# A two-layer hybrid decoder trunk on one core: four edits to its seams — low parts first in the opening, memory rows by halves of the contraction, the last output columns in two banks, queries scaled on ScalarE

## The chip, the core and the metric

One NeuronCore of a Trainium2 chip runs the whole program. The metric is the device time of one execution in microseconds (us), lower is better. Engines are named as in the profile: PE (TensorE, matrix products), ACT (ScalarE), DVE (VectorE), POOL (GpSimd) and SP (SyncE, which issues nearly all DMAs).

## The reference, cut to what matters

A sequence of 256 tokens of width 1024 goes through two layers, all in float32:

```python
for layer in range(2):
    x = x + 0.5 * swiglu(rms_norm(x), w_gate, w_up, w_down)      # 1024 -> 2816 -> 1024
    h, mem_n = rms_norm(x), rms_norm(mem)                        # mem: 256 rows of 1024
    mix = mlstm_mixer(h, mem_n, ...) if layer == 0 else dilated_mixer(h, mem_n, k_sh, v_sh, ...)
    x = x + mix                                                  # both hold a memory cross-attention
    x = x + 0.5 * swiglu(rms_norm(x), w_gate, w_up, w_down)
    if layer == 0: k_sh, v_sh = normed keys, values of rms_norm(x) @ w_kv
```

The memory cross-attention normalises queries and keys per head (4 heads of 64), takes a softmax over the 256 memory rows, and multiplies by the memory's values. Keys and values are `mem_n @ w_mem_kv`, 512 columns. The mLSTM mixer has 4 heads, the dilated mixer 12 heads in 3 groups.

## The kernel before, in words

**Exact products from split operands.** Each float32 weight and each activation is split into a high part (rounded to the fast float32 form that TensorE takes) and a low part, the remainder. ACT writes the high part (`hi`, a cast), DVE the low part (`lo`, a subtraction). A product of a 128x128 block with up to 512 columns is three matmuls into one PSUM bank: high with low, high with high, low with high (`mm3`, lines 561 to 566). In the trace the first name behind the arrow is the weight (`hi` or `lo`), the second the activation (`xh`, `xl`).

**Weight units.** `_stream` (line 54) lists all weights in the order of use, as units of at most 128 x 1024. SP loads a unit into one of 6 `raw` buffers, ACT and DVE split it into one of 8 ring slots (`RING`), and PE uses it twice, once for each half `t` of the 256 tokens. `release` (line 547) counts the uses and frees slots in the order of the stream only: a unit that is held keeps the slots of all units behind it.

**The planner.** No hardware scheduler orders the program. While it is recorded, a small model of the engines (`_Model`, line 167) keeps a clock for each engine, and side jobs (`spawn`: activations, norms, softmax, transposes) are recorded into the engines' queues when that clock says they are due. Each engine then runs its queue in order and waits on semaphores. `PAUSE` (line 38) is a number of microseconds that the planner adds between the scaling of a softmax row on DVE and its transposes on PE; it is not a wait on the chip.

**Opening.** The first product (`opening`, line 741) has nothing to hide behind: for each of 8 blocks `k` of the contraction it casts x's two halves (`xh`), casts the weights (`hi`), then records on DVE the weights' low part and x's two low parts (`xl`), and six matmuls. Unit 0 comes in two loads of half the width (`parts`, line 490), the others in one.

**Memory.** `memory` (line 71) puts six units in the stream behind the fifth feed-forward block: two of the transposed memory (`memT`, one for each half of the memory's rows, all 8 contraction blocks in each; POOL multiplies a gain into them) and four of weights (`mkv`, two contraction blocks each). `memory_kv` (line 910) goes over the four weight units, and in each over both halves of rows `m`, with one PSUM bank for each half. The bank is taken over from the feed-forward block before (`bank_of`). `keys` then norms the keys (ACT squares, DVE sums, POOL takes the power -1/2, DVE scales), and PE transposes them (`tpk`).

**Queries.** `query_rms` (line 686) serves both mixers: ACT squares the projected queries out of PSUM, DVE scales them into SBUF (`qn`), PE transposes them (`tpq`). Two PSUM banks (`tp`) serve all transposes, four (`acc`) the accumulators and scores, two (`mm`) the projections.

**End.** Every feed-forward ends in `dn` (line 867): eleven blocks accumulate into two banks of 512 columns for each half of tokens; after the last block DVE adds half of the bank to x, and SP stores 128 x 512 of the output. For the second half of tokens the last two products are those of columns 512 to 1023.

Of the kernel before, what the change touches and what calls it, by code (L numbers as in the profile page):

```python
# [17 lines left out]
P = 128  # L18
D = 1024
# [18 lines left out]
PAUSE = 1.0  # L38
# [13 lines left out]
def _stream():  # L52
# [285 lines left out]
class _Kernel:  # L338
# [151 lines left out]
    def parts(self, i):  # L490

        n = self.units[i][2]
        return [slice(0, n // 2), slice(n // 2, n)] if i == 0 else [slice(0, n)]

    def emit_unit(self):
# [6 lines left out]
        def steps(raw):  # L502
            if key[0] == "memT":
                raw3 = raw.rearrange("p (k t) -> p k t", k=NK)
                self.nc.gpsimd.tensor_tensor(
                    raw3, raw3, self.gains[7 + key[1]].unsqueeze(2).to_broadcast([P, NK, P]), ALU.mult)
                yield
# [178 lines left out]
    def query_rms(self, src, n, q, out, rstd):  # L686
# [5 lines left out]
        nc.vector.tensor_scalar(q, src, rstd, None, ALU.mult)  # L692
# [49 lines left out]
    def opening(self, ps, key):  # L742
# [4 lines left out]
        for k in range(NK):  # L747
# [14 lines left out]
            nc.vector.tensor_tensor(wl, raw[:, s], wh.bitcast(F32), ALU.subtract)  # L762
            for t, (hi, lo) in enumerate(parts):
                nc.vector.scalar_tensor_tensor(lo, x[:, t * P:(t + 1) * P], g, hi.bitcast(F32),
                                               ALU.mult, ALU.subtract)
            for t, (hi, lo) in enumerate(parts):
                self.matmul(ps[t], hi, wh, k == 0, False)
            for t, (hi, lo) in enumerate(parts):
                self.matmul(ps[t], hi, wl, False, False)
            for t, (hi, lo) in enumerate(parts):  # L770
                self.matmul(ps[t], lo, wh, False, k == NK - 1)
# [25 lines left out]
    def ffn_in(self, layer, which, after, memory, fp):  # L797
# [68 lines left out]

        def dn(b, t):
            if len(acc) == t:
# [6 lines left out]
            pairs = [(c, h) for h in range(2) for c in range(2)] if last else \  # L875
                    [(c, h) for c in range(2) for h in range(2)]
            for n, (c, h) in enumerate(pairs):
                wh, wl = self.get("dn", layer, which, b, c)
                self.until(max(self.model.ready(a) for a in (wl, parts[c][1])))
                f = slice(h * 512, (h + 1) * 512)  # L880
                self.mm3(acc[t][h], parts[c], (wh[:, f], wl[:, f]),
                         b == 0 and c == 0, last and c == 1)
                if last and n % 2:
                    nc.vector.scalar_tensor_tensor(self.x[t][:, f], acc[t][h], 0.5, self.x[t][:, f],
                                                   ALU.mult, ALU.add)
                    after(t, h)
                if h == 1:
# [33 lines left out]
    def memory_kv(self, layer, pool):  # L921
# [22 lines left out]
        ps, xT = [], []  # L944
        for k in range(0, NK, 2):
            for m in range(2):
                if k == 0:
                    ps.append(self.bank_of(m))
                    xT.append([a.rearrange("p (k t) -> p k t", k=NK)
                               for a in self.get("memT", layer, m)])  # L950
                hi, lo = xT[m]
                wh, wl = self.get("mkv", layer, k)
                self.until(self.model.ready(wl))
                for j in range(2):
                    s = slice(j * 512, (j + 1) * 512)
                    self.mm3(ps[m], (hi[:, k + j, :], lo[:, k + j, :]), (wh[:, s], wl[:, s]),
                             k + j == 0, k + j == NK - 1)
                self.release("mkv", layer, k)
                if k + 2 == NK:
                    self.release("memT", layer, m)  # L960
                    self.holder[m] = self.spawn(keys(m)(ps[m]))
                    chains.append(self.holder[m])
                self.tick()
# [534 lines left out]
    def run(self, stop=None):  # L1498
# [41 lines left out]
        def store(t, h):  # L1540
            f = slice(h * 512, (h + 1) * 512)
# [35 lines left out]
def _arrays(inputs):  # L1577
# [16 lines left out]
    w["memT"] = np.ascontiguousarray(w["mem"][0].reshape(2, P, NK, P).transpose(0, 3, 2, 1)).reshape(2 * P, D)  # L1594
# [23 lines left out]
```

## Time and profile before

| | |
|---|---|
| time, median of 3 runs | 1000.31 us (1000.02 to 1000.97) |
| the profiled execution: time / span of its instructions | 1000.46 us / 998.7 us |
| PE busy | 984.3 us, 99% of the span, clock 1.0 throughout |
| DVE / ACT / POOL busy | 628.3 / 550.3 / 65.0 us |
| DMA | 205 MB, mean 205 GB/s |

The span runs from the first instruction to the last; the profiled execution's time has 1.8 us more around it. A row of the timeline has a start, a duration, the engine, the line and the tiles; a bracket at its end tells how long the engine had been idle before it, and who ended that. Matmuls overlap: a row of 128x512 lasts 0.39 us, but the next one starts 0.23 us after it, and "idle" counts only from the modelled end.

### The profile page before, as it was taken

What the parts mean: (1) busy time and instruction counts of PE and PEld (TensorE: products, weight loads), DVE (VectorE), ACT (ScalarE), POOL (GpSimd) and SP (SyncE); (2) the same over time, 40 slices, a digit from 0 to 9 for tenths busy, and PEclk for the clock granted to TensorE, in tenths of its full rate; (3) what the DMA queues carried; (4) which work ended last, traced back from release to release, by engine and by line L of the source; (5) the groups of instructions that cost most, each with busy time, mean ns of one, the idle gap of its engine ahead of it and who ended that gap; (6) DMA issues with size and microseconds to landing.
All of it is one profiled execution on the core that took longest, in us unless ns stands there. A gap on an engine that the chain in (4) does not pass through costs nothing.

```text
span 998.7 us, 12959 instructions
## 1 busy us (share of the span) xinstructions
PE 984.3 (99%) x4673; PEld 814.2 (82%) x4673; DVE 628.3 (63%) x922; ACT 550.3 (55%) x853; POOL 65.0 (7%) x82
## 2 busy tenths in 40 slices
PE   9999999999999999999999999999999899999998
PEld 6887888898998888888877888788887688888886
DVE  5855656567967755556568563765567875665652
ACT  7655545478785644535377554554556585453541
POOL 0002000010010000000023010200012000000000
PEclk9999999999999999999999999999999999999999
DMA  9966867355446667676538675867551346767651
GB/s 361 306 207 219 292 225 216 118 158 196 153 149 210 199 224 259 207 246 206 199 109 305 232 237 174 290 206 253 175 192 64 106 161 219 263 208 242 211 172 42
DMA packets 80008, 205.05 MB, mean 205 GB/s; under 512 B 7564, under 2 KB 28744, under 8 KB 79944
## 3 DMA queue, kind: packets, MB, share of 16 engines
q1 hardware_dynamic: 79800, 204.20, 61.0%
q8 instruction: 36, 0.59, 0.2%
q14 instruction: 28, 0.23, 0.1%
q10 hardware_dynamic: 144, 0.04, 0.0%
HBM read 193.17 MB, written 11.03 MB: 204 GB/s over the span
## 4 chain that ended last, share of the span: by engine, by line
PE 82%; DVE 3%; POOL 2%; ACT 2%; issue 1%; DMA 1%; DVEq 0%; ACTq 0%
PE gups L567 42%; PE acc L567 22%; PE aps L567 7%; PE oacc L567 3%; PE kvps L567 2%; PE bqps L567 2%; DVE lo L277 1%; PE tps L574 1%; POOL rp_r L277 1%; DVE s L277 1%; PE sc L567 1%; PE po L567 1%; DMA hd<-hb 1%; POOL rp_e L277 1%; PE tpp L574 0%
## 5 line engine op out<-in xcount | busy, mean ns | idle before, releaser
L277 DVE TENSOR_TENSOR lo<-raw,hi 128x1024 fp32r<-128x1024 f32 (+3 forms) x351 | 407.1, 1181 | 125.9 <-ACT hi L277 119.3
L277 ACT CAST hi<-raw 128x1024 fp32r<-128x1024 f32 (+3 forms) x351 | 350.6, 1019 | 143.7 <-PE acc L567 84.4
L567 PE MATMUL gups<-lo,xh 128*128 128x512 f32 x704 | 273.8, 391 | 0.9 <-DVE lo L277 0.9
L567 PE MATMUL gups<-hi,xh 128*128 128x512 f32 x704 | 272.9, 389 | 1.0 <-ACT hi L277 1.0
L567 PE MATMUL gups<-hi,xl 128*128 128x512 f32 x704 | 272.7, 389 | 0.0
L567 PEld LDWEIGHTS gups<-lo,xh 128*128 128x128 f32 x704 | 132.0, 188 | 29.5 <-DVE lo L277 1.6
L567 PEld LDWEIGHTS gups<-hi,xh 128*128 128x128 f32 x704 | 132.0, 188 | 29.1 <-ACT hi L277 2.2
L567 PEld LDWEIGHTS gups<-hi,xl 128*128 128x128 f32 x704 | 132.2, 188 | 27.7
L277 ACT ACTIVATE sil<-gups,rstd 128x256 f32<-128x256 f32 x88 | 41.6, 474 | 163.9 <-PE gups L567 159.3
L277 DVE SCALAR_TENSOR_TENSOR h<-gups,rstd,sil 128x256 f32<-128x256 f32 x88 | 42.2, 481 | 123.6 <-ACT sil L277 123.5
L567 PE MATMUL acc<-lo,hhb 128*128 128x512 f32 x304 | 119.6, 393 | 0.0
L567 PE MATMUL acc<-hi,hlb 128*128 128x512 f32 x304 | 118.5, 390 | 0.0
L567 PE MATMUL acc<-hi,hhb 128*128 128x512 f32 x304 | 118.3, 389 | 0.0
L567 PEld LDWEIGHTS acc<-hi,hlb 128*128 128x128 f32 x304 | 57.1, 188 | 12.0
L567 PEld LDWEIGHTS acc<-hi,hhb 128*128 128x128 f32 x304 | 57.1, 188 | 11.4
L567 PEld LDWEIGHTS acc<-lo,hhb 128*128 128x128 f32 x304 | 57.1, 188 | 11.3
L567 PE MATMUL aps<-lo,xh 128*128 128x384 f32 (+1 forms) x144 | 49.5, 344 | 0.0
L567 PE MATMUL aps<-hi,xh 128*128 128x384 f32 (+1 forms) x144 | 47.5, 330 | 0.0
L567 PE MATMUL aps<-hi,xl 128*128 128x384 f32 (+1 forms) x144 | 47.5, 330 | 0.0
L277 DVE STREAM_TRANSPOSE hb<-h 128x256 f32<-128x256 f32 x76 | 33.6, 442 | 15.5 <-DMA hd<-hb 14.5
L277 POOL TENSOR_SCALAR rstd<-ss 128x1 f32<-128x1 f32 x12 | 3.6, 303 | 500.1 <-ACT junk L277 500.1
L277 ACT CAST hhb<-ht 128x512 fp32r<-128x512 f32 x38 | 23.6, 621 | 20.2 <-DMA ht<-hd 19.5
(189 smaller groups left out, 1012.9 us busy)
## 6 DMA issues: line engine op xcount, KB each, us to landing
raw<-in_wts SPq DMA_DIRECT2D x311, 512.0 KB, 4.7
raw<-in_wts SPq DMA_DIRECT2D x32, 384.0 KB, 3.8
hd<-hb SPq DMA_DIRECT2D x38, 256.0 KB, 5.3
ht<-hd SPq DMA_DIRECT2D x38, 256.0 KB, 4.6
bias<-diag SPq DMA_DIRECT2D x1, 1536.0 KB, 7.2
xraw<-in_xT SPq DMA_DIRECT2D x4, 256.0 KB, 6.2
x<-in_x SPq DMA_DIRECT2D x2, 512.0 KB, 8.5
mt<-in_mem SPq DMA_DIRECT2D x2, 512.0 KB, 6.9
```

The source lines that it names most:

```text
L277: call(out, *args, **kw)
L567: self.pe.matmul(out, lhsT=lhsT, rhs=rhs, start=start, stop=stop)
L574: self.pe.transpose(out, in_, ident)
```

## The change

Four edits and a number.

1. `opening`: DVE does x's low parts ahead of the weights' low part, and PE takes the products in the order that fits; unit 1 is loaded in two halves too.
2. `memory` and `memory_kv`: a `memT` unit now holds four contraction blocks of all 256 rows, and is followed in the stream by the two weight units that it meets. Each half of the contraction is finished for both halves of rows before the next.
3. `dn`: in the last feed-forward, for the second half of tokens, columns 512 to 1023 close their bank one block earlier and are added to x; the last block's product goes to two new banks of 256 columns, each with its own addition and store.
4. `query_rms`: queries are scaled on ACT instead of DVE.
5. `PAUSE` is 1.5 instead of 1.0.

```diff
-PAUSE = 1.0
+PAUSE = 1.5
     def memory(layer):
-        for m in range(2):
-            units.append((("memT", layer, m), ("memT", None, None, m, 1), D))
-        single(("mkv", layer), "w_mem_kv", layer, 0, 512, 2)
+        for q in range(2):
+            units.append((("memT", layer, q), ("memT", None, None, q, 1), D))
+            for k in range(4 * q, 4 * q + 4, 2):
+                units.append((("mkv", layer, k), (None, layer, (("w_mem_kv", 0, 512),), k, 2), 1024))
...
-        return [slice(0, n // 2), slice(n // 2, n)] if i == 0 else [slice(0, n)]
+        return [slice(0, n // 2), slice(n // 2, n)] if i < 2 else [slice(0, n)]
...
-        nc.vector.tensor_scalar(q, src, rstd, None, ALU.mult)
+        nc.scalar.activation(q, src, AF.Copy, scale=rstd)
...
             nc.scalar.copy(wh, raw[:, s])
-            nc.vector.tensor_tensor(wl, raw[:, s], wh.bitcast(F32), ALU.subtract)
             for t, (hi, lo) in enumerate(parts):
                 nc.vector.scalar_tensor_tensor(lo, x[:, t * P:(t + 1) * P], g, hi.bitcast(F32),
                                                ALU.mult, ALU.subtract)
+            nc.vector.tensor_tensor(wl, raw[:, s], wh.bitcast(F32), ALU.subtract)
...
+            groups = [(slice(h * 512, (h + 1) * 512), acc[t][h], b == 0, last) for h in range(2)]
+            if (layer, which, t) == (1, 2, 1) and b >= NB - 2:
+
+                f, a, begins, _ = groups.pop()
+                if last:
+                    self.freed_bank(*self.holder)
+                    add(t, f, a)
+                    for lo in (512, 768):
+                        bank = self.mm.tile([P, 512], F32, tag="mm", name="end")
+                        groups.append((slice(lo, lo + 256), bank[:, :256], True, True))
+                else:
+                    groups.append((f, a, begins, True))
...
+        for q in range(2):
+            hi, lo = (a.rearrange("p (k t) -> p k t", k=4) for a in self.get("memT", layer, q))
             for m in range(2):
...
+                for k in range(4 * q, 4 * q + 4, 2):
+                    wh, wl = self.get("mkv", layer, k)
...
+                    self.release("mkv", layer, k)
...
+            self.release("memT", layer, q)
```

The planner turns these edits into other orders. Three places, in the order in which each engine's queue holds its instructions:

The first instructions of DVE in the opening, before and then now; `lo` is the weights' low part, `xl` x's low part for one half of the tokens.

```order
L277 TENSOR_TENSOR lo_150<-raw_113,hi_149 128x512
L277 SCALAR_TENSOR_TENSOR xl_146<-xraw,gains,xh_145 128x128
L277 SCALAR_TENSOR_TENSOR xl_148<-xraw,gains,xh_147 128x128
L277 TENSOR_TENSOR lo_150<-raw_113,hi_149 128x512
L277 SCALAR_TENSOR_TENSOR xl_146<-xraw,gains,xh_145 128x128
```

```order
L278 SCALAR_TENSOR_TENSOR xl_147<-xraw,gains,xh_146 128x128
L278 SCALAR_TENSOR_TENSOR xl_149<-xraw,gains,xh_148 128x128
L278 TENSOR_TENSOR lo_151<-raw_113,hi_150 128x512
L278 SCALAR_TENSOR_TENSOR xl_147<-xraw,gains,xh_146 128x128
L278 SCALAR_TENSOR_TENSOR xl_149<-xraw,gains,xh_148 128x128
```

The two `xl`, which need only the casts of x, now stand ahead of `lo`, which needs the cast of the weights.

ACT around the memory block of layer 1, before and then now. `sil` is the last activation of the feed-forward block ahead of it, `vm` and `sq` are the values and squares of the memory's two halves of rows, `hi` are casts of weight units (the three now put in are those of the next feed-forward block), `hhb` is a cast of hidden activations.

```order
L277 ACTIVATE sil<-gups,rstd 128x256
L277 CAST hi_5656<-raw_5531 128x1024
L277 ACTIVATE vm<-mkvps,memr_90 128x256
L277 ACTIVATE sq<-mkvps,memr_90 128x256
L277 CAST hhb<-ht 128x4x4x32
L277 CAST hi_5715<-raw_5555 128x1024
L277 ACTIVATE vm<-mkvps,memr_91 128x256
L277 ACTIVATE sq<-mkvps,memr_91 128x256
L277 CAST hi_5760<-raw_5568 128x1024
```

```order
L278 ACTIVATE sil<-gups,rstd 128x256
L278 CAST hi_5657<-raw_5531 128x1024
L278 CAST hi_5688<-raw_5555 128x1024
L278 CAST hi_5691<-raw_5569 128x1024
L278 CAST hi_5703<-raw_5617 128x1024
L278 ACTIVATE vm<-mkvps,memr_90 128x256
L278 ACTIVATE sq<-mkvps,memr_90 128x256
L278 ACTIVATE vm<-mkvps,memr_91 128x256
L278 ACTIVATE sq<-mkvps,memr_91 128x256
L278 CAST hi_5748<-raw_5633 128x1024
```

Three casts of weights moved from behind the memory's last product to its middle; the same is so in layer 0, and DVE's three `lo` follow them.

PE in the attention of layer 1, where the last query projection (`bqps`) ends, before and then now. `tpp` are transposes of softmax rows (`s`, or `mp` for the memory), `po` products with values, `tpq` transposes of queries, `pa` and `pb` scores of the second half of tokens, `oacc` the output projection.

```order
L567 MATMUL bqps<-hi_6716,xl_6689 128x512
L574 MATMUL tpp<-consts,s 128x128 x6
L567 MATMUL po<-pTb,vs 64x128 x6
L574 MATMUL tpq<-consts,qn 128x128 x4
L574 MATMUL tpp<-consts,s 128x128 x6
L567 MATMUL po<-pTb,vs 64x128 x6
L574 MATMUL tpq<-consts,qn 128x128 x4
L567 MATMUL oacc_7049<-lo_6832,xh_6819 128x512
```

```order
L569 MATMUL bqps<-hi_6717,xl_6690 128x512
L576 MATMUL tpq<-consts,qn 128x128 x4
L569 MATMUL bqps<-lo_6718,xh_6689 128x512
L569 MATMUL bqps<-hi_6717,xh_6689 128x512
L569 MATMUL bqps<-hi_6717,xl_6690 128x512
L576 MATMUL tpp<-consts,s 128x128 x12
L569 MATMUL po<-pTb,vs 64x128 x6
L576 MATMUL tpq<-consts,qn 128x128 x4
L569 MATMUL po<-pTb,vs 64x128 x6
L569 MATMUL pa<-kTs,qTb_6704 128x256 x5
L569 MATMUL pb<-kTs,qTb_6704 128x256
L576 MATMUL tpp<-consts,mp 128x128 x4
```

All four softmax rows of the first half of tokens are now transposed in one piece, the first `tpq` stands ahead of them, and the scores `pa`, `pb` of the second half come ahead of the output projection.

## Rows read from the trace of the kernel before

**Rows 1.** Busy time of each engine in three stretches (mixer A, memory of layer 1, attention of layer 1).

```profile
core 0: us, PE busy (x) PEld busy (x) DVE busy (x) ACT busy (x) POOL busy (x), PEclk, DMA share, GB/s
...
195.00:325.00 130.00, 129.57 (x759) 117.40 (x758) 97.78 (x193) 99.44 (x181) 12.00 (x27) 1.00 0.51 167
600.00:640.00 40.00, 38.52 (x170) 31.03 (x169) 23.82 (x31) 21.23 (x28) 7.14 (x4) 1.00 0.63 211
738.00:815.00 77.00, 72.24 (x452) 55.89 (x451) 58.77 (x117) 50.35 (x108) 10.46 (x12) 1.00 0.33 111
```

**Rows 2.** Timeline of the opening: start, duration, engine, tiles, idle before.

```profile
7.44 0.70 ACT L277 ACTIVATE xh<-xraw,gains 128x128 fp32r<-128x128 f32 x2 [1.03 <-DMA xraw<-in_xT]
7.58 0.62 PE L567 MATMUL gups<-lo,xh 128*128 128x512 f32 x2
...
8.03 0.61 PE L567 MATMUL gups<-hi,xl 128*128 128x512 f32 x2
...
8.77 0.62 ACT L277 CAST hi<-raw 128x512 fp32r<-128x512 f32 x1 [0.63 <-DMA raw<-in_wts]
...
9.44 0.73 PE L567 MATMUL gups<-hi,xh 128*128 128x512 f32 x2 [0.79 <-ACT hi L277]
...
10.16 0.74 PE L567 MATMUL gups<-lo,xh 128*128 128x512 f32 x2
```

**Rows 3.** DMA rate in 40 slices of 0.75 us, from 0 to 30 us.

```profile
GB/s 0 0 84 248 393 331 205 388 339 361 410 361 418 423 415 415 421 426 421 415 414 406 431 426 415 410 426 426 421 415 415 421 431 240 120 213 350 180 235 360
```

**Rows 4.** Timeline of PE in and behind the two memory blocks.

```profile
75.14 0.50 PE L567 MATMUL mkvps<-lo,hi 128*128 128x512 f32 x1 [0.23 <-DVE h L277]
...
90.01 0.39 PE L567 MATMUL acc<-hi,hlb 128*128 128x512 f32 x1
90.79 0.47 PE L567 MATMUL gups<-lo,xh 128*128 128x512 f32 x1 [0.39 <-DVE lo L277]
...
93.10 0.50 PE L567 MATMUL gups<-lo,xh 128*128 128x512 f32 x1 [0.46 <-DVE lo L277]
...
632.08 0.44 PE L574 MATMUL tpk<-consts,kn 128*128 128x128 f32 x2 [1.17 <-DVE kn L277]
```

**Rows 5.** Timeline of ACT, DVE and POOL behind the memory blocks (layer 1, then 0).

```profile
618.89 0.47 ACT L277 ACTIVATE vm<-mkvps,memr 128x256 f32<-128x256 f32 x1 [8.71 <-PE mkvps L567]
...
622.53 4.84 ACT L277 CAST hi<-raw 128x1024 fp32r<-128x1024 f32 x5
...
625.46 4.62 DVE L277 TENSOR_TENSOR lo<-raw,hi 128x1024 fp32r<-128x1024 f32 x4
...
626.44 4.03 POOL L277 TENSOR_SCALAR rp_e<-hss 128x4 f32<-128x4 f32 x1
...
92.04 1.87 POOL L277 TENSOR_TENSOR rp_r<-rp_e,mhalf 128x4 f32<-128x4 f32 x1
```

**Rows 6.** Timeline of PE in the attention of layer 1.

```profile
783.91 0.50 PE L567 MATMUL oacc<-hi,xl 128*128 128x512 f32 x1 [1.59 <-DVE xl L277]
...
797.65 0.77 PE L567 MATMUL po<-mp,vm 128*64 128x128 f32 x10 [0.97 <-ACT mp L277]
```

**Rows 7.** Groups of instructions from 738 to 815 us: xcount | busy us, mean ns.

```profile
L277 ACT ACTIVATE sq<-bqps,rstd 128x512 f32<-128x512 f32 x4 | 2.8, 690 | 1.3 <-PE bqps L567 1.3
...
L277 DVE TENSOR_SCALAR qn<-bqps,rstd 128x512 f32<-128x512 f32 x4 | 3.0, 749 | 4.6 <-ACT sq L277 4.5
```

**Rows 8.** Timeline at the end of the program.

```profile
994.79 0.39 PE L567 MATMUL acc<-hi,hl 128*128 128x512 f32 x1
995.21 0.69 DVE L277 SCALAR_TENSOR_TENSOR x<-acc,x 128x512 f32<-128x512 f32 x1 [0.67 <-PE acc L567]
```

**Rows 9.** Chain of waits near 205 us, sixteen matmuls of 264 columns.

```profile
204.92 2.16 PE aps L567 x16
```

**Rows 10.** The same DVE operation on 256 columns, a group of the page.

```profile
L277 DVE SCALAR_TENSOR_TENSOR h<-gups,rstd,sil 128x256 f32<-128x256 f32 x88 | 42.2, 481 | 123.6 <-ACT sil L277 123.5
```

**Rows 11.** DMA rate in 40 slices, 995.0 to 998.7 us.

```profile
GB/s 0 0 0 0 177 376 443 443 399 399 376 200 22 0 0 0 0 0 0 266 487 421 376 376 421 354 133 0 0 0 0 0 0 0 0 0 0 0 0 0
```

More of the change, by code (lines that the diff above doesn't have):

```diff
@@ L874, in dn @@
             last = b == NB - 1
-            pairs = [(c, h) for h in range(2) for c in range(2)] if last else \
-                    [(c, h) for c in range(2) for h in range(2)]
-            for n, (c, h) in enumerate(pairs):
-                wh, wl = self.get("dn", layer, which, b, c)
[L879 to L887, printed above, removed]
+            groups = [(slice(h * 512, (h + 1) * 512), acc[t][h], b == 0, last) for h in range(2)]
[9 more added lines that the diff above has]
+                    groups.append((f, a, begins, True))
+            pairs = [(c, q) for q in groups for c in range(2)] if last else \
+                    [(c, q) for c in range(2) for q in groups]
+            for c, (f, a, begins, ends) in pairs:
+                wh, wl = self.get("dn", layer, which, b, c)
+                self.until(max(self.model.ready(i) for i in (wl, parts[c][1])))
+                self.mm3(a, parts[c], (wh[:, f], wl[:, f]), begins and c == 0, ends and c == 1)
+                if last and c == 1:
+                    add(t, f, a)
+                    after(t, f if f.stop - f.start < 512 else f.start // 512)
+                if f.stop == D:
                     self.release("dn", layer, which, b, c)
@@ L942, in keys @@
             return steps
-        ps, xT = [], []
-        for k in range(0, NK, 2):
+        ps = []
+        for q in range(2):
+            hi, lo = (a.rearrange("p (k t) -> p k t", k=4) for a in self.get("memT", layer, q))
             for m in range(2):
-                if k == 0:
+                if q == 0:
                     ps.append(self.bank_of(m))
[L949 to L960, printed above, removed]
+                t = slice(m * P, (m + 1) * P)
+                for k in range(4 * q, 4 * q + 4, 2):
+                    wh, wl = self.get("mkv", layer, k)
+                    self.until(self.model.ready(wl))
+                    for j in range(2):
+                        s = slice(j * 512, (j + 1) * 512)
+                        i = k + j - 4 * q
+                        self.mm3(ps[m], (hi[:, i, t], lo[:, i, t]), (wh[:, s], wl[:, s]),
+                                 k + j == 0, k + j == NK - 1)
+                    self.release("mkv", layer, k)
+                    self.tick()
+                if q == 1:
                     self.holder[m] = self.spawn(keys(m)(ps[m]))
                     chains.append(self.holder[m])
-                self.tick()
+            self.release("memT", layer, q)
         return kmT, vm, chains
@@ L1540, in store @@
         def store(t, h):
-            f = slice(h * 512, (h + 1) * 512)
+            f = h if isinstance(h, slice) else slice(h * 512, (h + 1) * 512)
             nc.sync.dma_start(self.out[0, t * P:(t + 1) * P, f], self.x[t][:, f])
```

14 lines of the change are left out of this document (9 added, 5 removed).

## The prediction, written before the changed kernel ran

> **What bounds the kernel now.** I read the page's first table first: PE is busy 984.3 of the span's 998.7 us at full clock, so no other engine's work counts unless PE waits for it. What can be won is the 14 us in which PE has nothing, less what start and end need. Next the busy time by stretch [rows 1]. In mixer A PE lacks 0.43 us of 130 (130.00 − 129.57), in the memory of layer 1 it lacks 1.48 of 40, in the attention of layer 1 it lacks 4.76 of 77, with ACT busy 50.35 and DVE 58.77. Last the timelines, for where PE's idle brackets stand in the stretches that the edits touch: the opening [rows 2], the memory blocks [rows 4, 5], the attention [rows 6] and the end [rows 8]. The number of matmul columns stays the same everywhere, so every term below is a wait of PE removed, added or moved.
>
> A bracket understates a loss. Two matmuls of a running stream start 0.45 us apart, 8.03 − 7.58 [rows 2], so one takes 0.23; but a row lasts 0.39 to 0.5, and idle counts from its end. Where I have the row before, I count start to start.
>
> **The change part by part.** The sum is made against the profiled execution, 1000.46 us (span 998.7 and 1.8 around it), which lies 0.15 above the median of 1000.31.
>
> *Opening.* ACT has done x's casts at 7.44 + 0.70 = 8.14 and waits until 8.77 for unit 1's weights [rows 2]; PE, which could have gone on at 8.03 + 0.45 = 8.48, starts at 9.44, a loss of 0.96. Loaded in two halves, the part that block 1 needs is 256 KB earlier at the 361 to 410 GB/s of that time [rows 3], 0.67 us, which covers ACT's wait of 0.63. I take −0.6. x's low parts first: the products at 9.44 and 10.16 start 0.72 apart instead of 0.45, since the weights' low part comes last; that is −0.27, of which I take −0.2, as part may wait on the next load anyway. The added load is one more issue on SP, hidden by the transfers queued there: the rate is level near 415 GB/s from 9 to 23 us [rows 3], so the queue never runs dry. Together −0.8; bounds −1.23 (both losses whole) and 0 (the half lands with the whole).
>
> *Memory of layer 0.* Three waits behind it are of one kind: DVE's `lo` for the next feed-forward comes late, because units held to the end of the memory's 48 products keep the ring full. They are 90.01 to 90.79 (0.78 − 0.23 = 0.55), 0.46 at 93.10, and ahead of them 0.23 plus 0.16 of hidden start-to-start time, 0.39, at 75.14, where the bank of the second half of rows is taken over too late [rows 4]. Now three slots come free at product 24 of 48, 24 × 0.23 = 5.5 us sooner, and ACT, which idles 8.71 us in the same place of layer 1 [rows 5], casts then. The second bank is needed after 12 products (2.7 us), not after 6 (1.4), so 0.39 goes as well. I take −1.4, bounds −1.4 and −0.4 (only the bank). What moves is three casts of 0.97 (4.84 / 5) and three `lo` of 1.16 (4.62 / 4) [rows 5], all inside 5.5 us of ACT's and DVE's idle time. If that cover were gone, `vm` and `sq` would queue behind 2.9 us of casts on ACT, and the next bank taker, a feed-forward block, would wait for them.
>
> *Memory of layer 1.* Of the 1.48 idle in the window, 1.17 stand before `tpk` at 632.08 [rows 1, 4]. The chain is: normed keys `kn` on DVE, before them a power on POOL (`rp_e`) that lasts 4.03 us from 626.44, beside four `lo` that run on DVE from 625.46 to 630.08 [rows 5]. With three `lo` gone from there, POOL's step should be short and `kn` early. I take −1.5, bounds −1.7 (the whole idle, plus the 0.2 that brackets hide) and −0.4 (only the bank). The POOL step is where a page bears. The Trainium skill, "SBUF — State Buffer", section "Who interferes with whom", has it that a DVE instruction with two SBUF inputs contends with a GpSimd instruction that reads SBUF, and that the loser blocks for the whole instruction. The 4.03 beside four `lo` agrees; the 1.87 of `rp_r` behind layer 0's memory [rows 5] shows that such a step need not be that long. By the rule POOL stays exposed to any `lo` that the planner puts beside it, and that is a rival below.
>
> *Mixer A.* Queries leave DVE for ACT, and the transposes are rearranged. PE lacks 0.43 there [rows 1], the most that can be won. The most that I see lost is two queries with some 0.47 each (the time of a 256-wide `vm`, [rows 5]) on ACT ahead of something PE waits for, 0.94; DVE (97.78) and ACT (99.44) are three quarters busy, so either can hide it. I take 0.
>
> *Attention of layer 1.* Four `qn` leave DVE (749 ns each, 3.0 us) and four of about the same as `sq`, 690 ns, join ACT [rows 7]. Four `qn` on path would be +2.8 at worst; −1.8 is the best (1.59 before `oacc` at 783.91 and part of the rest). PE's largest waits are 1.59 for DVE's `xl` and 0.97 for ACT's `mp` [rows 6]. The first should shrink: with `pa` and `pb` ahead of `oacc` there is scoring work between, and DVE is 0.75 lighter. Against it, twelve `tpp` stand in one piece, and need the two `tp` banks in turn; ACT must empty them, with `sq` and the new `qn` (2 × 0.69 = 1.4) between its copies, so one wait of about 0.8 appears. And `mp` is an ACT step behind these. I take −1.6 for `xl`, +0.8 for the banks, +0.3 for `mp`: −0.5, bounds −1.8 and +2.8. `PAUSE` acts only through these orders.
>
> *End.* The path is last product, addition, store. The addition falls from 0.69 [rows 8] to 0.48 [rows 10], −0.21; the last matmul has half the columns, −0.1; the last store moves half the bytes, 131 KB at about 400 GB/s [rows 11], −0.33. Twelve products of 256 columns replace six of 512: at most 0.135 each (2.16 / 16 for 264 columns, [rows 9]) make 1.6 against 1.4, +0.2. Together −0.45, bounds −0.7 and 0. The earlier store of 256 columns is issued 0.8 us sooner, and lands before.
>
> Sum: −0.8 − 1.4 − 1.5 + 0 − 0.5 − 0.45 = −4.65. 1000.46 − 4.65 = 995.8; against the median 995.66. I say 995.7.
>
> **The rivals.** A measurement of this kernel can tell about 0.2%, 2 us, from no change.
>
> *POOL still blocked.* `lo` of the next units stand beside `rp_e` in the new order too, since the next feed-forward goes on casting; then layer 1's memory gives −0.4, not −1.5, and the time is 996.8. For it: 4.03 us against 1.87 in a like place [rows 5]. Against: the second half of the memory now holds fewer slots, so the casts are spread out. Chance 0.15, faster still.
>
> *The attention takes it back.* ACT gets 2.8 us more in a stretch where PE already waits for it (`mp` 0.97). If each of the four falls on the path, +2.8 replaces −0.5: 995.7 + 3.3 = 999.0. Against: ACT is busy 50.35 of 77 [rows 1], and there PE has other work queued. Chance 0.17, of which 0.12 count as within 0.2% and 0.05 (2 on the path) as faster.
>
> *Slower.* The `tp` banks become the bound of the attention. Some 20 groups of transposes go through two banks there; if each copy out stands behind a `qn` by half of its 0.69, 0.35, that is +7, and with nothing of the −0.5: 996.2 + 7 = 1003.2. It decides from 300 ns for each group. Against: the largest part of the groups are softmax rows, away from the queries. In the windows, PE's idle of 4.76 would be near 11. Chance 0.05.
>
> *The opening's half gives nothing.* The two halves may travel side by side. If the first half of unit 1 lands where the whole did, the opening gives −0.2 and the time is 996.3. It lies in the forecast's own range.
>
> **How the numbers follow.** Forecast 0.63, POOL 0.15, attention 0.17, slower 0.05. The forecast's own range: best, opening −1.2 and attention −1.8, 994.0; worst, opening 0, end −0.2, layer 0 −1.0: 997.2. For 8 in 10 I go down to 993.6 (mixer A's 0.43 added) and up to 998.9, which takes in POOL's case and nearly all of the attention's. Faster is the forecast (0.63, of which 0.03 may fall short of 2 us), POOL's 0.15 and 0.05: 0.80. Within 0.2%: 0.12 + 0.03 = 0.15. Slower 0.05.
>
> **What the profile after would show.** Opening: ACT's bracket at 8.77 gone, PE's third pair near 8.8, the pair behind it 0.45 later. Memory: no ACT bracket of 8.71 before `vm`, three casts in its place; in layer 0 no brackets for `lo` in the 4 us behind it; in layer 1 no 1.17 before `tpk`, and `rp_e` under 2 us. Attention: the 1.59 before `oacc` gone, a new bracket before `tpp` or `po` of about 0.8, idle of the window near 4.3. End: an addition of 0.48 and two small stores. The forecast is wrong if the window of the attention lacks more than 7 us, if `rp_e` stays at 4 us and `tpk` waits for it, or if waits for `lo` turn up one block later, since then the ring's total rate, not its held slots, was the cause.

## The result, and the profile after

| | before | after |
|---|---|---|
| time, median of 6 runs each | 999.59 us | 992.35 us |
| profiled execution: time / span | 1000.46 / 998.7 us | 992.88 / 990.4 us |
| PE busy | 984.3 us | 980.8 us |

The ratio of the times is 0.9929, 95% interval 0.9916 to 0.9941. In a second comparison on one chip it was 0.9935 (0.9923 to 0.9948): 998.91 to 992.52, −6.4 us. The forecast was 995.7, with a range down to 993.6: the direction was right, and the kernel is faster than the range allowed.

Where the time went is read best between two matmuls that stand in both traces. Both spans, cut at the starts of such matmuls (us):

| stretch, from and to | before | after | difference |
|---|---|---|---|
| opening: start to the 49th `gups` | 18.01 | 17.00 | −1.01 |
| memory of layer 0: first `mkvps` to the 265th `gups` | 24.07 | 22.59 | −1.48 |
| mixer A: first `aps` to first `oacc` | 97.93 | 97.05 | −0.88 |
| memory of layer 1: 49th `mkvps` to the 1341st `gups` | 29.03 | 26.79 | −2.24 |
| attention of layer 1: first `bqps` to the 1585th `gups` | 76.46 | 73.99 | −2.47 |
| end: last `gups` to the end | 17.83 | 17.51 | −0.32 |
| all else | 735.43 | 735.49 | +0.06 |

The total is −8.3, more than the timed −6.4 to −7.2; the experiments show that two rows of the table, the opening and the memory of layer 1, are larger here than in other executions of the same code.

Busy time of each engine by stretch, of the kernel after (columns as in [rows 1]):

```profile
195.00:325.00 130.00, 129.88 (x764) 117.53 (x764) 97.34 (x191) 98.58 (x182) 11.98 (x27) 1.00 0.52 171
600.00:640.00 40.00, 40.00 (x180) 33.05 (x179) 27.34 (x34) 23.58 (x30) 3.25 (x4) 1.00 0.71 240
732.00:807.00 75.00, 71.19 (x454) 56.00 (x453) 56.63 (x112) 52.76 (x112) 9.42 (x12) 1.00 0.37 124
```

Against [rows 1] PE's idle fell from 1.48 to 0 in the memory of layer 1, from 4.76 to 3.81 in the attention, and from 0.43 to 0.12 in mixer A. These are smaller falls than the table's. The rest of the gain lies in PE's busy time, which fell by 3.5 us in all although no matmul column was removed: the tail of a matmul that nothing follows counts as busy (0.39 against a pitch of 0.23, so 0.16 for each wait). PE has 22 idle brackets of any length before and 12 after, so tails are about 1.6 of the 3.5 us; the rest is not traced to its place here. The Trainium skill, "Perfetto Trace Analysis", in the note ahead of its sections, calls matmul busy time a bad metric for judging how close a kernel is to its roofline, because matmuls are pipelined; this trace agrees, by those 3.5 us.

Timeline of the opening after:

```profile
5.08 1.22 PE L569 MATMUL gups<-hi,xh 128*128 128x512 f32 x2
6.10 1.03 PE L569 MATMUL gups<-hi,xl 128*128 128x512 f32 x2
6.96 0.65 PE L569 MATMUL gups<-lo,xh 128*128 128x512 f32 x2
7.45 0.62 PE L569 MATMUL gups<-hi,xh 128*128 128x512 f32 x2
8.12 0.60 ACT L278 CAST hi<-raw 128x512 fp32r<-128x512 f32 x1
```

ACT's bracket at 8.77 and PE's 0.79 at 9.44 [rows 2] are gone (ACT waits 0.82 for the next load at 10.14, where PE has work). But behind the pairs at 5.08 and 6.10 the next one starts 1.02 and 0.86 later, about twice the 0.45 that a pair takes at full pitch. The `PEclk` column reads 1.00 there, but it counts time without a record as full clock: the trace's record of the granted clock begins only at 6.98 us, and there the pitch goes from 0.43 to 0.23. (In the kernel before it begins at 4.97, ahead of the first `gups`; "clock 1.0 throughout" holds from there on.)

ACT, then POOL, in the memory of layer 1 after (start, duration):

```profile
609.56 3.14 ACT L278 CAST hi<-raw 128x1024 fp32r<-128x1024 f32 x3 [2.61 <-PE mkvps L569]
613.64 0.47 ACT L278 ACTIVATE vm<-mkvps,memr 128x256 f32<-128x256 f32 x1 [0.94 <-PE mkvps L569]
...
616.55 0.19 POOL L278 TENSOR_SCALAR rp_e<-hss 128x4 f32<-128x4 f32 x1 [27.41 <-DVE hss L278]
616.83 1.01 POOL L278 TENSOR_TENSOR rp_r<-rp_e,mhalf 128x4 f32<-128x4 f32 x1
618.14 0.19 POOL L278 TENSOR_SCALAR rp_e<-hss 128x4 f32<-128x4 f32 x1 [0.30 <-DVE hss L278]
```

The three casts now stand in ACT's idle stretch of 8.71 [rows 5], and `rp_e` takes 0.19 instead of 1.10 and 4.03. PE waits for no `tpk` here.

PE's waits in the attention, first those of before that [rows 6] does not show, then those after:

```profile
766.66 1.25 PE L567 MATMUL po<-pTb,vs 128*64 128x128 f32 x12 [0.60 <-ACT pTb L277]
...
769.28 0.55 PE L574 MATMUL tpp<-consts,s 128*128 128x128 f32 x3 [0.45 <-ACT qTb L277]
770.03 0.43 PE L567 MATMUL po<-pTb,vs 128*64 128x128 f32 x2 [0.20 <-ACT pTb L277]
...
775.54 0.66 PE L574 MATMUL tpp<-consts,mp 128*128 128x128 f32 x4 [0.35 <-ACT mp L277]
...
796.25 0.43 PE L567 MATMUL po<-mp,vm 128*64 128x128 f32 x2 [0.28 <-ACT mp L277]
```

```profile
762.39 0.55 PE L576 MATMUL tpp<-consts,s 128*128 128x128 f32 x3 [0.99 <-ACT pTb L278]
...
775.45 0.88 PE L576 MATMUL tpp<-consts,s 128*128 128x128 f32 x6 [1.14 <-DVE s L278]
...
788.66 0.47 PE L569 MATMUL oacc<-lo,xh 128*128 128x512 f32 x1 [0.79 <-DVE x L278]
...
799.07 0.50 PE L569 MATMUL oacc<-lo,xh 128*128 128x512 f32 x1 [0.46 <-ACT xh L278]
```

The 1.59 and 0.97 of [rows 6] are gone, and the forecast wait of the `tp` banks is there (0.99). The longest wait is now 1.14.

The end after:

```profile
985.86 0.69 DVE L278 SCALAR_TENSOR_TENSOR x<-acc,x 128x512 f32<-128x512 f32 x1 [0.67 <-PE acc L569]
...
986.57 0.43 DVE L278 SCALAR_TENSOR_TENSOR x<-end,x 128x256 f32<-128x256 f32 x1
...
986.97 0.28 PE L569 MATMUL end<-hi,hl 128*128 128x256 f32 x1
987.29 0.42 DVE L278 SCALAR_TENSOR_TENSOR x<-end,x 128x256 f32<-128x256 f32 x1 [0.29 <-PE end L569]
```

From the last matmul to the end of the span it was 3.9 us [rows 8] (994.79 to 998.7), and is 3.4 (986.97 to 990.4).

### The profile page after: what moved, and what is told of

The parts are those of the page before. It is cut to its first block, busy times and chain, and to the rows that moved or that the text cites. A ratio compares the mean times of both kernels' runs of the same rounds, so it can differ in the third digit from the quotient of the medians.

```text
span 990.4 us, 12979 instructions
## 1 busy us (share of the span) xinstructions
PE 980.8 (99%) x4679; PEld 814.9 (82%) x4679; DVE 629.0 (64%) x918; ACT 551.8 (56%) x858; POOL 59.9 (6%) x82
## 4 chain that ended last, share of the span: by engine, by line
PE 85%; DVE 2%; ACT 2%; POOL 1%; issue 1%; DVEq 0%; ACTq 0%
PE gups L569 43%; PE acc L569 22%; PE aps L569 7%; PE oacc L569 3%; PE kvps L569 2%; PE bqps L569 2%; PE mkvps L569 1%; PE tps L576 1%; POOL rp_r L278 1%; DVE s L278 1%; PE sc L569 1%; ACT hi L278 1%; DVE lo L278 0%; PE pn L569 0%; ACT xh L278 0%
```

## The experiments

Each kernel ran in five rounds beside the kernel before on the same chip. The kernel before had medians of 999.10 beside the four single edits, 999.87 beside queries alone, `PAUSE` alone, held slots and one operand, 998.91 beside the kernel after, its two variants without one edit and the zeros, and 999.23 beside the last four. A difference in us is the difference of medians; the interval is that of the ratio.

**Each edit by itself.** The memory edit alone:

```diff
+        for q in range(2):
+            units.append((("memT", layer, q), ("memT", None, None, q, 1), D))
+            for k in range(4 * q, 4 * q + 4, 2):
+                units.append((("mkv", layer, k), ...))
...
```

Here and below, `...` stands for lines or arguments left out.

> The kernel before with the memory edit alone. Theory (each wait counted from start to start, in the two traces): layer 0 gives 1.5 us, layer 1 gives 2.1 to 2.2, nothing elsewhere: -3.6 us against the kernel before, with the waits at 75.14, 90.79, 93.10 and 632.08 gone and PE idle near 0 from 600 to 640 us. Rival (the brackets are the whole loss, as I forecast): -2.9. Second rival (part of the attention's gain comes from the memory edit through the planner): -4 or more, with a changed attention.

Ratio 0.9976 (0.9967 to 0.9984), −2.5 us: less than the theory, near the first rival's −2.9. By the trace the memory of layer 0 fell to 22.61 and that of layer 1 to 26.79, as in the kernel after, and the other stretches stayed, apart from the opening (18.49, see below). So the trace's −3.6 was right for the stretches it compared, but that of layer 1 was unusually long in the profile of before (below).

The opening edit alone:

```diff
-        return [slice(0, n // 2), slice(n // 2, n)] if i == 0 else [slice(0, n)]
+        return [slice(0, n // 2), slice(n // 2, n)] if i < 2 else [slice(0, n)]
...
-            nc.vector.tensor_tensor(wl, raw[:, s], wh.bitcast(F32), ALU.subtract)
             for t, (hi, lo) in enumerate(parts):
...
+            nc.vector.tensor_tensor(wl, raw[:, s], wh.bitcast(F32), ALU.subtract)
...
```

> The kernel before with the opening edit alone (unit 1 in halves, x's low parts first). Theory: -1.0 us, all of it before 11 us of the span. Rival: the gain is eaten later, because the loads behind the opening come no earlier; then the trace shows a wait of PE between 11 and 60 us and the time is within 0.3 of before.

Ratio 1.0001 (0.9992 to 1.0009), 0 us. The theory failed. The 49th `gups` came at 16.96, as in the kernel after, but the next 36 took 8.81 us instead of 8.52, and the memory of layer 0 24.47 instead of 24.07; the rival had the time, and in part the reason.

Queries on ACT and `PAUSE` 1.5:

```diff
-PAUSE = 1.0
+PAUSE = 1.5
...
-        nc.vector.tensor_scalar(q, src, rstd, None, ALU.mult)
+        nc.scalar.activation(q, src, AF.Copy, scale=rstd)
```

> The kernel before with queries scaled on ACT and PAUSE 1.5, nothing else. Theory (these two give all that the attention and mixer A gained): -2.5 in the attention of layer 1 and -0.6 in mixer A, together -3.1 us, with the attention's waits as in the changed kernel: about 1.2 before the twelve tpp, 1.1 before the next tpp, 0.8 before an oacc, 0.5 behind the last po. Rival (the attention gains because the memory edit leaves ACT and DVE freer): under -1.5.

Ratio 0.9974 (0.9965 to 0.9982), −2.9 us. The attention took 73.97 and mixer A 97.07, as in the kernel after: the theory holds, and these stretches owe nothing to the memory edit.

The last columns in two banks, alone (the hunk of `dn`):

```diff
+                    for lo in (512, 768):
+                        bank = self.mm.tile([P, 512], F32, tag="mm", name="end")
+                        groups.append((slice(lo, lo + 256), bank[:, :256], True, True))
```

> The kernel before with the last columns in two banks, nothing else. Theory: -0.3 us as the two traces show (forecast -0.45): the last matmul, a shorter addition (0.48 instead of 0.69) and half the bytes. Rival: the two added stores queue behind each other and nothing is won: 0.

Ratio 0.9996 (0.9985 to 1.0006): the times can't tell. The trace shows 17.47 instead of 17.83, −0.36.

**Queries and `PAUSE` apart.** Only the line of `query_rms`, and then only the number (the two parts of the diff of queries and `PAUSE`):

> The kernel before with queries scaled on ACT alone (PAUSE stays 1.0). Theory: moving the queries off DVE is what takes away the 1.59 before oacc (DVE's xl late), so the attention gains 1.5 or more by it alone. Rival: the gain is the planner's order under PAUSE 1.5, and this run gives under 0.7, or loses because ACT's copies stand behind the scalings.

> The kernel before with PAUSE 1.5 alone. Theory (queries matter): within 0.7 us of before in the attention. Rival (order matters): -1.5 or more there, with the 1.59 before oacc gone although qn is still on DVE.

Queries alone: ratio 0.9985 (0.9976 to 0.9993), −1.6 us; the attention takes 74.90, −1.56, the expected size, but not by the expected wait: 0.69 of the 1.59 for `xl` is left, the waits of 0.97 and 0.28 for `mp` stay, and a third one for `mp` grows from 0.35 to 1.25. Mixer A takes 98.16, +0.23. `PAUSE` alone: 0.9989 (0.9979 to 0.9999), −1.3 us; mixer A takes 96.87, −1.06, but the attention 77.69, +1.23. Neither expectation foresaw that, though half of the rival came: the 1.59 is gone while `qn` is still on DVE, so the order alone removes it. PE in the attention of the run with queries alone:

```profile
779.89 0.49 PE L567 MATMUL oacc<-hi,xl 128*128 128x512 f32 x1 [0.69 <-DVE xl L277]
```

PE in the attention of `PAUSE` alone, and the busy time there:

```profile
781.50 1.54 PE L574 MATMUL tpp<-consts,s 128*128 128x128 f32 x6 [2.66 <-DVE s L277]
...
783.69 0.63 PE L567 MATMUL oacc<-hi,xl 128*128 128x512 f32 x1
784.12 0.63 PE L567 MATMUL oacc<-lo,xh 128*128 128x512 f32 x1
```

```profile
776.00:782.00 6.00, 3.34 (x31) 2.32 (x30) 5.93 (x9) 3.73 (x7) 0.00 (x0) 0.89 0.47 156
782.00:788.00 6.00, 6.00 (x22) 4.98 (x21) 4.03 (x9) 2.51 (x8) 0.00 (x0) 0.54 0.59 204
```

With the longer `PAUSE` a softmax row comes late from DVE, which is busy 5.93 of the 6 us, PE waits 2.66 us for it, and behind that wait the granted clock is at half, the 1.2 GHz level: 0.54 over the six us, and matmuls start 0.43 apart instead of 0.23. The wait seems to be paid twice.

**Is the clock a price of its own?** `PAUSE` 1.5 alone, with products of zeros put where PE waited:

```diff
                     tp = yield from self.psum("tp", [P, 4, P], "tpp")
+                    for _ in range(11 if (t, j, lo) == (1, 0, 0) else 0):
+                        self.pe.matmul(tp.rearrange("p a b -> p (a b)"), lhsT=self.warm[:, :P],
+                                       rhs=self.warm, start=True, stop=True)
...
```

> PAUSE 1.5 alone, as in the run before of that kind, with eleven products of zeros put into the transposes' free bank where PE waited 2.66 us for s; the order of all else is the same. Theory (the wait costs twice, once as idle time and once because the granted clock falls to 0.5 behind it): PE is as late at the transposes of s, but the clock stays 1.0 behind them, and the attention falls from 77.69 to about 75.7; -2.0 us against PAUSE 1.5 alone. Rival (the clock falls for another reason, or the added products delay the transposes): 77.5 or more.

The attention fell to 75.82, −1.87, as the theory said. Timeline and busy time of PE in the same place:

```profile
777.53 2.55 PE L1436 MATMUL tpp<-warm 128*128 128x512 bf16 x11
780.25 0.88 PE L574 MATMUL tpp<-consts,s 128*128 128x128 f32 x6 [0.17 <-DVE s L277]
...
781.66 0.39 PE L567 MATMUL oacc<-lo,xh 128*128 128x512 f32 x1
781.89 0.39 PE L567 MATMUL oacc<-hi,xh 128*128 128x512 f32 x1
```

```profile
776.00:782.00 6.00, 5.83 (x40) 3.50 (x37) 5.89 (x12) 4.01 (x8) 0.00 (x0) 1.00 0.64 198
782.00:788.00 6.00, 5.62 (x52) 4.29 (x51) 4.36 (x10) 3.27 (x10) 0.00 (x0) 1.00 0.39 152
```

The row of `s` comes no earlier behind `ms` than before (2.5 us of zeros, then 0.17 of waiting), but the clock stays at 1.00 and the matmuls 0.23 apart. In these two profiles a wait of 2.66 us cost some 4.5 (2.66 and 1.87). The first of them had the lowest clock of the eleven executions with `PAUSE` alone: a mean of 0.997, against 0.998 in eight and 0.999 in two; so 4.5 is the upper end. The times do not show the gain: ratio 0.9985 (0.9976 to 0.9994) against 0.9989 (0.9979 to 0.9999) for `PAUSE` alone, two intervals that overlap, on two chips.

**The two of them inside the kernel after.** Queries on DVE again with `PAUSE` 1.5; then `PAUSE` 1.0 with queries on ACT; beside the kernel after itself:

> The changed kernel again, beside more runs of the kernel before. Theory (the single edits add up, -2.5 memory, 0 opening, -2.85 queries and PAUSE, 0 end, -5.3 together, the rest is which chip ran): -5 to -5.5 us, and a profile whose attention and mixer A repeat those of the first one within 0.1. Rival (the edits help each other): -6.5 to -7.5.

> The changed kernel with queries scaled on DVE again, PAUSE still 1.5. Theory (PAUSE 1.5 without the query edit makes a softmax row so late that PE waits 2.66 us and its clock falls): the attention takes 77 to 78 us instead of 74, PE waits over 2 us for s near 774 and the granted clock is 0.5 behind it; +3 to +4 us over the changed kernel. Rival (that wait came from the memory edit being absent): under +1.5.

> The changed kernel with PAUSE 1.0 again. Theory (each as in its own run): mixer A +1.1 (98.16 instead of 97.05) and attention +0.9 (74.90 instead of 73.99): +2.0 us over the changed kernel, the two waits in front of tpc (0.43) and po (0.97) back. Rival (PAUSE matters only with the old queries): under +0.7.

The kernel after: −6.4 us (0.9935, 0.9923 to 0.9948), at the edge of the rival's range and above the sum of the four single runs (−2.5, +0.2, −2.9, +0.1: −5.1); with four intervals of about ±0.9 us each the two can't be told apart. Queries on DVE: 994.75, +2.2 over the kernel after (ratio to before 0.9955, 0.9942 to 0.9969); PE waits 2.65 for `s` at 778.75 and the attention takes 76.45. That is the theory's mechanism at the low end: in this profile the clock came back after four slow matmuls instead of nine, and in two of the five executions the mean clock was 1.00. `PAUSE` 1.0: 994.63, +2.1 (0.9958, 0.9946 to 0.9971), with mixer A at 98.12 and the attention at 74.95: as expected.

**Held slots or order of products.** The memory edit alone, with the slots given back only at its end:

```diff
-            self.release("memT", layer, q)
+        for q in range(2):
+            self.release("memT", layer, q)
         return kmT, vm, chains
```

> The memory edit alone, but both memT units are given back only at the end of the memory's products, so that the ring's slots stay held as in the kernel before; the products keep the new order (halves of the contraction). Theory (held slots cause the late lo): of the 3.6 us of the memory edit only the bank waits come (0.39 + 0.47 = 0.9 us); the waits for lo at 90.79 and 93.10 and the one before tpk in layer 1 stay. Rival (the order of the products is what matters): the whole 3.6.

Ratio 1.0001 (0.9991 to 1.0011): nothing of the memory edit's gain is left. PE and its clock in layer 0:

```profile
91.04 0.47 PE L569 MATMUL gups<-lo,xh 128*128 128x512 f32 x1 [1.77 <-DVE lo L278]
...
94.37 0.63 PE L569 MATMUL gups<-hi,xl 128*128 128x512 f32 x1
94.80 0.63 PE L569 MATMUL gups<-lo,xh 128*128 128x512 f32 x1
```

```profile
88.00:92.00 4.00, 2.20 (x9) 1.21 (x7) 2.72 (x5) 3.24 (x5) 0.39 (x2) 1.00 0.06 9
92.00:96.00 4.00, 3.79 (x11) 2.81 (x12) 4.00 (x5) 3.31 (x5) 2.08 (x2) 0.62 0.72 240
```

The late `lo` is back, longer (1.77) than in the kernel before, and the clock falls behind it: the stretch takes 26.34 instead of 22.6. So it is the early return of slots that pays, as the forecast had it. The 0.9 that I expected from the banks does not show in the time. In this profile the longer wait and the clock behind it cost more than that; but in seven of the twelve executions the mean clock was 1.00, and their median, 1000.0, is no better than that of before either, so the clock alone does not account for it.

**What holds POOL.** The kernel before, with another DVE instruction for eight low parts behind the memory of layer 1, which are so left out of the result:

```diff
-            self.nc.vector.tensor_tensor(lo[:, :width], raw[:, :width],
-                                         hi.bitcast(F32)[:, :width], ALU.subtract)
+            if key[:4] == ("gu", 1, 1, 5) or key[:4] in (("dn", 1, 1, 2), ("dn", 1, 1, 3)):
...
+                v.engine.tensor_scalar(lo[:, :width], full, 2.0 ** -12, 0.0, ALU.mult, ALU.add, accum_out=sums)
...
+            else:
+                self.nc.vector.tensor_tensor(lo[:, :width], raw[:, :width],
+                                             hi.bitcast(F32)[:, :width], ALU.subtract)
```

> The kernel before, but the eight units behind the memory of layer 1 get their low part from a DVE instruction that reads one SBUF operand (the high part times a constant, summed beside) instead of two; so those low parts are left out of the result. The order on every engine is the same. Theory (POOL is blocked by DVE instructions with two SBUF inputs): rp_e at 626.44 falls from 4.03 us to about 0.2 to 0.3, the second kn comes right behind the first, and the 1.17 before tpk goes (-1.2 us, about -1.2 in all). Rival (DVE's queue, where kn stands behind four lo, is the cause): rp_e may change, the wait before tpk stays over 0.8.

POOL there with two-operand `lo` beside it, in the run with only the end changed, and then with one-operand `lo`:

```profile
623.40 1.10 POOL L277 TENSOR_SCALAR rp_e<-hss 128x4 f32<-128x4 f32 x1 [36.12 <-DVE hss L277]
...
625.67 0.29 POOL L277 TENSOR_SCALAR rp_e<-hss 128x4 f32<-128x4 f32 x1
626.04 1.87 POOL L277 TENSOR_TENSOR rp_r<-rp_e,mhalf 128x4 f32<-128x4 f32 x1
```

```profile
622.81 0.19 POOL L277 TENSOR_SCALAR rp_e<-hss 128x4 f32<-128x4 f32 x1 [35.04 <-DVE hss L277]
623.09 1.01 POOL L277 TENSOR_TENSOR rp_r<-rp_e,mhalf 128x4 f32<-128x4 f32 x1
624.28 0.19 POOL L277 TENSOR_SCALAR rp_e<-hss 128x4 f32<-128x4 f32 x1 [0.18 <-DVE hss L277]
624.55 1.01 POOL L277 TENSOR_TENSOR rp_r<-rp_e,mhalf 128x4 f32<-128x4 f32 x1
```

DVE's instructions last the same (1.21 us against 1.22) in the same order; with one operand from SBUF POOL runs at its own 0.19 and 1.01. That is shown. But the first fence is the kernel before's own code, and there the second `rp_e` took 0.29, not 4.03: whether POOL gets in between two `lo` or waits for the whole row of them differs from one execution to the next. Of seven profiles of this code (the kernel before and the runs with the opening alone, the end alone, queries alone, `PAUSE` alone, queries and `PAUSE`, and the zeros) two had 4.03 (stretches of 29.0 and 28.6 us, with waits of 1.17 and 0.76 before `tpk`). Of the other five, four took 27.5 to 27.6 and one 28.7, where PE waited 0.68 for a late `lo` instead. The average is 28.1, where the new code takes 26.8. The time, 0.9988 (0.9978 to 0.9997), −1.0, fits the expected −1.2, yet the stretch took 27.95, with a bank wait of 0.86 ahead: how much the block costs on average stays open.

**Why the opening gives nothing.** The kernel after with the old opening, and with twelve instead of nine products of zeros ahead of the first product (`WARM`):

```diff
-WARM = 9
+WARM = 12
```

> The changed kernel with the old opening (unit 1 in one load, weights' low part first). Theory (the opening edit takes away waits for data but PE then runs its first products at twice the pitch, so nothing is left): within 0.5 us of the changed kernel. Rival (the edit gives the 0.8 to 1.0 that I forecast): +0.8 or more over the changed kernel.

> The changed kernel with twelve instead of nine products of zeros ahead of the opening, so that PE does not pause between them and the first product. Theory (the pause of up to 0.5 us there is why the first products of the changed kernel run at a pitch of 0.43): the first product starts near 6.4, all products run at 0.23 from then on, the opening's 48 products end near 17.4 in every execution, against 17.0 to 18.75; time 0 to -0.5 against the changed kernel. Rival (the pause is not the reason): the slow products stay, and the opening ends 0.5 to 1.3 later.

Old opening: 992.85, ratio to before 0.9935 (0.9923 to 0.9948), the kernel after's own ratio. Twelve products: 992.67, 0.9935 (0.9922 to 0.9949). The first products of the kernel after in its second profile, and with twelve products ahead:

```profile
5.75 1.22 PE L569 MATMUL gups<-hi,xh 128*128 128x512 f32 x2 [0.49 <-ACT hi L278]
6.78 1.05 PE L569 MATMUL gups<-hi,xl 128*128 128x512 f32 x2
7.63 1.05 PE L569 MATMUL gups<-lo,xh 128*128 128x512 f32 x2
...
10.10 0.63 PE L569 MATMUL gups<-lo,xh 128*128 128x512 f32 x2
10.57 0.62 PE L569 MATMUL gups<-hi,xh 128*128 128x512 f32 x2
```

```profile
1.24 4.40 PE L1527 MATMUL warm<-warm 128*128 128x512 bf16 x12 [1.24 <-DVE warm L278]
5.28 0.81 PE L569 MATMUL gups<-hi,xh 128*128 128x512 f32 x2
5.94 0.63 PE L569 MATMUL gups<-hi,xl 128*128 128x512 f32 x2
6.41 0.62 PE L569 MATMUL gups<-lo,xh 128*128 128x512 f32 x2
```

In that second profile of the same kernel eight matmuls run at 0.43 (three in the first), and the 49th comes at 18.75, not 17.00. Each time the slow pitch ends where the trace's record of the granted clock begins, 9.98 us in the second profile and 6.98 in the first. With twelve products PE is at 0.23 from 5.94 on and the 49th comes at 16.50; but that is given back, since the next 36 `gups` take 8.98 instead of 8.52, where PE now waits for `h`. This profile does not show the theory's reason: its clock record begins at 4.58, while the products of zeros still ran, so the pause ahead of the first product would have come too late to matter. Over ten profiles with the old opening the 85th `gups` starts at 25.5 to 27.0, on average 26.0; over seven with the new one and nine products of zeros at 25.3 to 27.3, also 26.0 on average.

Two things in these profiles bear on that. The wait of 0.79 at 9.44 [rows 2], from which the forecast took its gain, was late data in one execution: of the ten profiles with the old opening one other has such a wait (1.24), two have 0.26 and 0.09, and six none. And the clock record begins at 3.97 to 7.19 us in the nine profiles with the old opening that have one, but at 6.63 to 9.98 in the seven with the new one, so that there more of the products run at the slow pitch. Where the moments agree (7.19 in the run with one operand, old opening; 7.21 with `PAUSE` 2.0, new), the 85th `gups` starts at 25.57 and 25.60. So in that pair, with no late data in either, the edit brings nothing; elsewhere what it saves goes into slow products or later waits. What sets the moment at which the clock rises, and whether the edit moves it or chance did, stays open.

**Is `PAUSE` a rule?** The kernel after with 2.0 and with 1.75 in that line:

> The changed kernel with PAUSE 2.0. Theory (the number matters only through the orders it happens to give; 1.5 with queries on ACT leaves waits of 1.14, 0.98 and 0.79 in the attention): a new order, no better than chance; between -1 and +3 us against the changed kernel. If the wait for s near 774 grows past 2 us, the clock falls behind it and it is +3.

> The changed kernel with PAUSE 1.75. Theory as for 2.0, with a smaller change of order: between -0.7 and +2 us against the changed kernel, attention 73 to 76.

2.0: 994.42, ratio 0.9952 (0.9940 to 0.9965): mixer A takes 95.06, two less than at 1.5, but mainly because 16 of its 32 `po` and 8 of its 16 `tpp` now stand behind the first `oacc`; from the first to the last of its `oacc` it takes 27.08 instead of 23.32. 1.75: 992.53, 0.9931 (0.9919 to 0.9943), the attention at 73.59. Neither beats the kernel after beyond the measurement, and the number acts through the order it happens to give.

## Why the prediction was wrong

Averaged over all profiles that have a stretch's old or new code, the differences are: opening 0.0 (forecast −0.8), memory of layer 0 −1.45 (−1.4), memory of layer 1 −1.2 (−1.5), mixer A −0.9 (0), attention −2.5 (−0.5), end −0.3 (−0.45). They add up to −6.4, which is the timed −6.4 on one chip.

- **The step that failed is the attention's**: "I take −1.6 for `xl`, +0.8 for the banks, +0.3 for `mp`". The `xl` wait went, the bank wait came (0.99 and 0.24), both about as sized. But `mp` became no later: its waits (0.97, 0.35 and 0.28 in the same timeline of before) went, as did three before `tpp` and `po` (0.60, 0.45 and 0.20) and one of 0.29 at the end; I had counted none of these as removed. Of waits of 0.2 us and more, eight became five. In their place came 1.14, 0.79 and 0.46. I had priced one removed wait of eight, and the added ones that I feared. The lower bound, −1.8, was wrong by the same mistake: idle in the window was 4.76, and more than 1.8 of it was within reach. The reason given for the `xl` term, lighter work on DVE and scoring in between, holds only in part: queries on ACT alone leave 0.69 of that wait, the order under `PAUSE` 1.5 alone removes it whole, and neither alone gives −2.5 (−1.56 and +1.23). It is the two together that do.
- **The bound from idle time was wrong too**: "PE lacks 0.43 there [rows 1], the most that can be won", for mixer A. It gave 0.9: 0.8 less between the starts of `tpc` and what follows them, where the bracket was 0.43, and smaller differences both ways inside PE's busy time. I had said that a bracket understates a loss, and used it for the opening and layer 0 only. The run with `PAUSE` alone shows that the number, not the queries, brought this gain; the forecast gave it no price: "`PAUSE` acts only through these orders" was right and then not followed up.
- **Memory of layer 0**: right, step and size; the run with held slots shows the mechanism. A wait before `tpk` that the forecast did not have has come (0.36 in the first profile, 0.2 to 1.0 in the others).
- **Memory of layer 1**: the size came out, and POOL was rightly named, but for the wrong base. The profile before showed an execution in which POOL was held 4.03 us; in five of seven it was not, and against the four profiles at 27.5 the gain is 0.7. The gain over the average is −1.2, so the −1.5 is near it partly by luck.
- **Opening**: the term of −0.8 was nothing. The waits it names went (the bracket at 8.77, the late third pair), and the time did not follow: the wait of 0.79 was that of one execution, and with the new opening PE ran longer at the slow pitch. I had asked what hides the added load, not what is late next. The rival "the opening's half gives nothing" had the result but not the reason: the cast that the half feeds ends at 8.0 us on average over the seven profiles, against 8.9 over the ten with the old opening.
- **End**: right in kind. The addition of 256 columns takes 0.43, not the 0.48 I took from the nearest row.
- The rival of the slower side, two `tp` banks as the bound, did not come: the added `tpp` waits are 1.2 us in all, far from the 6 us (300 ns for each of some 20 groups) that it needed. The rival of POOL still blocked did not come either (`rp_e` 0.19), nor that of the queries on ACT's path.

The base helped the miss as well: the one profiled execution, 1000.46, lies 0.6 to 1.6 us over before's later medians (998.9 to 999.9).

## What to carry to other kernels

Price a removed wait from start to start of the instructions around it, and list every wait of the stretch that a new order touches, not only the largest: where the order changes, all of them are drawn anew. Before a wait seen in one profile is put into a sum, ask whether it is a race between two engines that another execution may win. And find the longest wait that is left: one that dropped TensorE's clock cost 1.7 times its length in the execution profiled here (4.5 us for 2.66).

## What the runs showed of the hardware

- Behind a wait of 2.66 us the granted clock was 0.50, the 1.2 GHz level, for nine matmuls (`PAUSE` alone), behind one of 2.65 for four (queries on DVE in the kernel after); in two of five executions of the latter the mean clock stayed 1.00. Behind one of 1.77 it was 0.62 over the next 4 us. In 69 runs of the kernel before on two chips the mean granted clock was 1.00 in 48, and 0.998 in 12, whose medians were 1.6 to 2.0 us longer; the kernel after, with 1.14 as its longest wait in the middle, had 1.00 in all 11. Which wait drops it in the kernel before no profile caught, but the runs point at the 1.59 before `oacc`: 0.998 or less came in 1 to 4 of 11 or 12 executions of each of the five other kernels that keep that wait (1.57 to 1.59; held slots has the 1.77 besides), and in none of the 69 executions of the nine kernels whose longest wait behind the opening is 1.38 or less.
- At the start of the program matmuls run at 0.43, the pitch of the 1.2 GHz level, until the trace's first record of the granted clock, and at 0.23 from there on. That moment was 3.97 to 9.98 us into the span in the 17 traces that have such a record (one has none); in two executions of the same kernel it was 6.98 and 9.98, with three and eight slow `gups`. The `PEclk` column reads 1.00 all the same, since it counts time without a record as full.
- A POOL instruction on 128x4 elements waited through four back-to-back DVE instructions with two SBUF operands in two executions (4.03 us), and took 0.28 to 0.29 us in the same place in five; beside DVE instructions with one SBUF operand it took 0.19.
